# A planner for a hybrid encoder: TensorE's clock priced by activity, split copies and elementwise work free to change engine, leads for each layer and attention block

## The chip, the core and the metric

The kernel runs on one core of a Trainium2 chip. The metric is device time in microseconds (us) of one launch. The engines are TensorE (PE; PEld is its weight load), VectorE (DVE), ScalarE (ACT), GpSimd (POOL) and SyncE (SP, which here only issues transfers).

## What is computed

Two layers of an encoder over 512 tokens of width 1024, all in float32. Each layer has a mixer stage and a feed-forward stage:

```python
h = rms_norm(x, norm_mix[l]); proj = h @ w_in[l]          # 1024 x 3224
y_att = banded window attention(q, k, v)                  # 6 heads, 4 blocks of 128 queries
y_dn  = gated DeltaNet, one scan per direction            # 6 heads, 8 chunks of 64
y_rw  = RWKV-7, one scan per direction                    # 4 heads, 8 chunks of 64
x = x + concat(y_att, y_dn, y_rw) @ w_out[l]
h = rms_norm(x, norm_ffn[l])
x = x + (silu(gate) * val) @ w_down[l]                    # gate, val = conv3(h @ w_up[l])
```

Both recurrences are computed by chunks: inside each chunk a triangular matrix is inverted, and a scan of 8 dependent steps follows. A last RMSNorm closes the trunk.

## The kernel before, in words

Tiles hold channels on 128 partitions and the 512 tokens along the free axis. A large product is made in three float32r passes: each operand is split into a high part (a copy that rounds) and a low part (source minus high), and high x high, low x high and high x low are summed in PSUM. For weights, `weights` (its tiles: `wr` as loaded, `wh` high, `wl` low) loads four 128x128 blocks at a time, copies them on ACT and subtracts on POOL; each of the three tiles has three buffers. For activations, `split` writes `hh` and `hl`; in the feed-forward stage the gated result is split into two halves of a `p`, `cv` or `at` tile. A product of width 1024 is 24 matmuls of 128x512 (8 blocks, 3 passes), one of width 2816 is 66.

The mixer of a layer runs, in the order in which the program records it: 9 projections with `token_shift` (RWKV's inputs); `rwkv_prep` for two head pairs; `dn_gates`; `dn_proj` 0 to 2 (three projections each, with a conv of five taps on DVE); `invert`, the first inversion, 62 dependent instructions on DVE; `finish_inverse` 0, its PE part; `rwkv_scan`; `attn_proj` and `dn_prep` 0 to 2 beside it; `rwkv_out`; `invert_both`, the second inversion, 65 instructions on DVE; `finish_inverse` 1 and 2; `dn_scan`; `attn_head` 0 to 2 (four blocks each) and `gate_proj` 0 to 2 as filling; `dn_out`. After it come the output projection (`w_out`) and the feed-forward stage (up, down).

Nothing runs in the recorded order. Every call goes to a `Plan` (`add`), which notes its engine, its cost by a formula (`price`), its dependences and the tiles that it needs. `schedule` then places all 12326 calls: it takes the engine that is free first, and on it the ready call of the highest priority, where priority is the longest chain of costs behind the call plus a lead of its group, `LEAD`. A group is one call of a task such as `dn_prep`; before, both layers share a lead. `emit` writes the calls in the planned order, and the engines run their queues in that order, each queue strictly in sequence. So the plan decides what stands in front of what; how long it takes is decided on the chip. Every instruction shows line L516, the recorder's.

Three rules of the planner matter here. `other` names a second engine that may run a call; `schedule` offers the call to both and the one that is free first takes it. `admit` lets a tile be opened early if the memory allows. And the PE model in `schedule` doubles a matmul's cost after the PE has been idle.

Of the kernel before, what the change touches and what calls it, by code (L numbers as in the profile page):

```python
# [7 lines left out]
F32 = mybir.dt.float32  # L8
F32R = mybir.dt.float32r
# [89 lines left out]
def _param_array(inputs):  # L99
# [27 lines left out]
    "token_shift": 631900,  # L127
# [7 lines left out]
class Plan:  # L135
# [3 lines left out]
    def __init__(self, nc):  # L139
# [3 lines left out]
        self.flexible = True  # L143
        self.group, self.count, self.per_layer, self.lead = None, {}, {"proj": 9, "finish_inverse": 3, "rwkv_prep": 2, "dn_prep": 3, "dn_proj": 3, "attn_head": 3, "gate_proj": 3, "rwkv_out": 2, "dn_out": 3}, LEAD
# [8 lines left out]
    def task(self, f):  # L153


        def started(*a, **k):
            mine = self.group is None
            if mine:
                n = self.count[f.__name__] = self.count.get(f.__name__, -1) + 1
                name = f"{f.__name__}{n % self.per_layer[f.__name__]}" if f.__name__ in self.per_layer else f.__name__  # L160
            else:
                name = self.group
# [8 lines left out]
            def steps():  # L171
                while True:
                    old, self.group = self.group, name
# [94 lines left out]
    def other(self, o, name, reads, writes):  # L268

        if not self.flexible or not writes or len(reads) < 1 or "float32r" in str(writes[0].dtype) or reads[0].dtype != F32:  # L270
            return None
        dst, src = o.args[0], o.args[1]
        n = int(np.prod(dst.shape[1:]))
        psum = str(src.space).endswith("PSUM")
# [5 lines left out]
        if o.eng == "DVE" and name == "tensor_copy":  # L280
            return "ACT", self.nc.scalar.activation, (dst, src, AF.Copy), {}, 190 + 0.85 * n
# [1299 lines left out]
```

## Time and profile before

| what | value |
|---|---|
| median of 3 runs (lowest, highest) | 1678.78 us (1677.74, 1680.12) |
| profiled execution, its own time | 1681.65 us |
| span of the profile, first to last instruction | 1679.5 us |
| granted TensorE clock, mean | 0.946 |
| busy: PE, DVE, ACT, POOL | 91%, 64%, 44%, 38% |

The profiled execution is 2.9 us above the median, and 2.15 us of its time lie outside the span. A granted clock of 1.00 is 2.4 GHz, 0.50 is 1.2 GHz; a value between is a mean over both levels. Busy time of an engine counts its instructions; how near a stage is to its limit is seen when the busy time of an engine is set against the length of the same stretch.

### The profile page before, as it was taken

To read this page: it belongs to the slowest core of one execution; us is meant where nothing else is said; L and a number is where in the kernel's file an instruction comes from. 1 tells how busy PE (TensorE), PEld (TensorE's weight loads), DVE (VectorE), ACT (ScalarE), POOL (GpSimd) and SP (SyncE) were. 2 spreads that over 40 slices of the span, in tenths; PEclk is the share of its full clock that TensorE was granted. 3 is DMA by queue.
4 is the path that set the end of the run, shared out by engine and by line. 5 is a ranking of instruction groups with operands and counts; after the bars stand their busy time and mean duration, and the time that the engine had idled before them with its cause. 6 is when DMAs were issued, how large, how long until landed. Compare 5 with 4: busy or idle time off the path is not lost. (4 is left out here: it accounts for less than half of the span.)

```text
span 1679.5 us, 29012 instructions
## 1 busy us (share of the span) xinstructions
PE 1531.1 (91%) x11500; PEld 1192.8 (71%) x11500; DVE 1083.1 (64%) x1689; ACT 736.2 (44%) x1399; POOL 645.2 (38%) x510
## 2 busy tenths in 40 slices
PE   7999787589999999999999996966899999999996
PEld 5677665367777777788876775644677877777885
DVE  7799977967437666740058998789654566766101
ACT  5565345454543433332236544355544433334221
POOL 5422332010555554555552232410017454555553
PEclk9999889779999999999999997996799999999998
DMA  6312303010233333333342121120003333333332
GB/s 177 84 34 76 70 20 89 13 34 2 71 91 100 94 89 95 94 106 112 108 105 64 47 75 39 54 86 1 27 14 89 94 88 95 95 93 88 115 91 85
DMA packets 230536, 126.07 MB, mean 75 GB/s; under 512 B 23656, under 2 KB 221416, under 8 KB 230400
## 3 DMA queue, kind: packets, MB, share of 16 engines
q1 hardware_dynamic: 228624, 121.02, 25.8%
q10 hardware_dynamic: 1776, 3.20, 0.7%
q8 instruction: 90, 1.47, 0.3%
q14 instruction: 46, 0.38, 0.1%
HBM read 117.84 MB, written 6.34 MB: 74 GB/s over the span
## 5 line engine op out<-in xcount | busy, mean ns | idle before, releaser
L516 POOL TENSOR_TENSOR wl<-wr,wh 128x512 fp32r<-128x512 f32 (+1 forms) x408 | 558.1, 1379 | 830.1 <-ACT wh L516 667.9
L516 PE MATMUL ps<-hh,wh 128*128 128x512 f32 x1248 | 457.6, 399 | 6.9 <-ACT wh L516 6.9
L516 ACT ACTIVATE wh<-wr 128x512 fp32r<-128x512 f32 (+1 forms) x408 | 243.5, 616 | 495.9 <-PE ps L516 433.9
L516 PE MATMUL ps<-hh,wl 128*128 128x512 f32 x1248 | 452.9, 398 | 7.4 <-POOL wl L516 5.3
L516 PE MATMUL ps<-hl,wh 128*128 128x512 f32 x1248 | 451.6, 394 | 0.0
L516 PEld LDWEIGHTS ps<-hh,wl 128*128 128x128 f32 x1248 | 232.7, 187 | 84.2 <-POOL wl L516 30.3
L516 PEld LDWEIGHTS ps<-hh,wh 128*128 128x128 f32 x1248 | 233.6, 188 | 69.8 <-ACT wh L516 16.2
L516 PEld LDWEIGHTS ps<-hl,wh 128*128 128x128 f32 x1248 | 233.8, 188 | 51.7 <-issue 3.4
L516 DVE TENSOR_TENSOR p<-ps,p 128x512 f32<-128x512 f32 (+2 forms) x72 | 38.2, 551 | 197.4 <-PE ps L516 197.1
L516 PE MATMUL ps<-p,wh 128*128 128x512 f32 x512 | 158.2, 389 | 0.0
L516 DVE TENSOR_TENSOR td<-ps,rb 128x512 f32<-128x512 f32 (+1 forms) x64 | 43.7, 688 | 136.4 <-PE ps L516 136.3
L516 PEld LDWEIGHTS ps<-p,wh 128*128 128x128 f32 x512 | 96.1, 188 | 19.9
L516 DVE SCALAR_TENSOR_TENSOR tr<-td,fixed,tr 128x511 f32<-128x511 f32 x88 | 105.3, 1197 | 0.6 <-ACT tr L516 0.4
L516 PE MATMUL ps<-p,wl 128*128 128x512 f32 x256 | 99.8, 390 | 0.0
L516 ACT ACTIVATE p<-p 32x256 f32<-32x256 f32 (+3 forms) x112 | 66.0, 589 | 16.1 <-DVE p L516 11.2
L516 PE MATMUL ps<-fixed,cv 128*128 128x128 f32 x168 | 36.6, 338 | 38.8 <-ACT cv L516 35.7
L516 DVE SCALAR_TENSOR_TENSOR td<-tr,fixed,td 128x511 f32<-128x511 f32 x88 | 70.8, 805 | 0.3
L516 PE MATMUL ps<-p,p 32*32 32x32 f32 (+2 forms) x1232 | 56.1, 253 | 14.9 <-DVE p L516 11.3
L516 DVE TENSOR_TENSOR tr<-tr,td 128x512 f32<-128x512 f32 x44 | 67.3, 1529 | 1.6
L516 ACT ACTIVATE p<-ps 64x256 f32<-64x256 f32 (+4 forms) x113 | 44.9, 401 | 52.7 <-PE ps L516 33.3
L516 PEld LDWEIGHTS ps<-sm,p 64*64 64x64 f32 x1344 | 49.4, 145 | 24.6 <-DVE sm L516 12.9
L516 PEld LDWEIGHTS ps<-p,p 32*32 32x32 f32 (+1 forms) x1232 | 51.3, 143 | 21.5 <-DVE p L516 12.1
(170 smaller groups left out, 2089.5 us busy)
## 6 DMA issues: line engine op xcount, KB each, us to landing
wr<-ffn_w_up SPq DMA_DIRECT2D x176, 256.0 KB, 2.8
wr<-w_in SPq DMA_DIRECT2D x88, 256.0 KB, 2.8
wr<-ffn_w_down SPq DMA_DIRECT2D x80, 256.0 KB, 2.9
p<-scr ACTq DMA_DIRECT2D x12, 256.0 KB, 5.1
wr<-w_in SPq DMA_DIRECT2D x24, 128.0 KB, 2.6
wr<-w_out SPq DMA_DIRECT2D x32, 96.0 KB, 2.6
wr<-w_out SPq DMA_DIRECT2D x16, 192.0 KB, 2.6
p<-xt SPq DMA_DIRECT2D x8, 256.0 KB, 4.5
```

The source lines that it names most:

```text
L516: tc.keep_in_program_order(call(*args, **kw))
```

## The change

It changes only the planner, its table of leads and one argument.

1. **The clock in the plan.** The rule "idle for over 5 us, then slow until enough full-width work is done" goes. Instead the plan books PE time by beats of fixed length, each matmul weighted by its kind, and doubles costs in a beat that follows one with too little. This changes the plan only; nothing on the chip is set.
2. **Who may change engine** (`other`). Before, a call that writes float32r could not. Now the high copies of weights and activations may go from ACT to DVE, and a `tensor_tensor` in SBUF with two dimensions and at least 128 elements in a row may go from DVE to POOL or back. The low part of the weights has three dimensions and stays on POOL.
3. **Leads** for each layer (`a`, `b`), and for each block of an attention head; `token_shift` 0 to 7 get their own.
4. `wake` puts a call that is still blocked back on the waiting list. `admit` tests the name instead of the size of a room; the rooms below 4 are the same three, so nothing changes by it. `bufs=2` to `bufs=1` in `split` has no effect: `Plan.tile` uses `bufs` only for tags in its `room`, and `hh` and `hl` are not among them.

```diff
 LEAD = {
-    "attn_head0": -17500, "attn_head1": 13500, "attn_head2": 4300, "attn_proj": 281000, "dn_gates": 100400, "dn_out0": 5100,
...
+    "attn_head0a.0": 28600, "attn_head0a.1": -100, "attn_head0a.2": -158900, "attn_head0a.3": 800, "attn_head0a.4": 1500, "attn_head0b.0": 50500,
...
@@ other
-        if not self.flexible or not writes or len(reads) < 1 or "float32r" in str(writes[0].dtype) or reads[0].dtype != F32:
+        if not writes or not reads:
             return None
...
-        if o.eng == "DVE" and name == "tensor_copy":
+        if o.eng == "DVE" and name == "tensor_copy" and src.dtype == F32:
...
+        if name == "tensor_tensor" and not psum and n >= 128 and len(dst.shape) == 2 and o.eng in ("DVE", "POOL"):
+            e, f, cost = ("POOL", self.nc.gpsimd, 180 + 2.3 * n) if o.eng == "DVE" else ("DVE", self.nc.vector, 165 + 1.04 * n)
+            return e, f.tensor_tensor, o.args, o.kw, cost
@@ schedule
-                if t - free[e] > self.COLD:
-                    cold, heat = True, 0.0
-                if cold:
+                while t >= edge:
+                    slow = here < (self.UP if slow else self.DOWN) * self.BEAT
+                    here, then, edge = then, 0.0, edge + self.BEAT
+                if slow:
                     cost *= 2
...
-            elif o.contend and e == "DVE" and free["POOL"] > t:
+            elif e == "DVE" and (o.contend or o.eng == "POOL") and free["POOL"] > t:
                 cost += min(cost, free["POOL"] - t)
```

The set of calls is the same in both kernels; 470 of ACT's calls now run on DVE (176 before), 60 of DVE's on POOL and 15 of POOL's on DVE. Three places show the new order.

**First, DVE in layer 0, between the RWKV scan and the second inversion.** `p_105` is RWKV's result (task `rwkv_out`), `p_538` to `p_541` belong to `dn_prep` 2. Before:

```order
L516 TENSOR_TENSOR p_538<-p_538,fixed 128x1024 x2
L516 TENSOR_TENSOR p_105<-p_105,tr_558 128x512
L516 TENSOR_SCALAR p_105<-p_105,fixed 128x512
L516 TENSOR_TENSOR p_105<-p_105,tr_553 128x512
L516 TENSOR_TENSOR p_105<-p_105,tr_554 128x512
L516 TENSOR_TENSOR cv_398<-cv_398,td_532 128x512
L516 SCALAR_TENSOR_TENSOR cv_408<-cv_408,td_533 128x512
```

DVE in the changed kernel:

```order
L544 TENSOR_TENSOR p_538<-p_538,fixed 128x1024 x2
L544 SCALAR_TENSOR_TENSOR cv_408<-cv_408,td_533 128x512
L544 COPY p_529<-ps_531 64x4x64 x3
L544 TENSOR_TENSOR p_540<-ps_542,p_538 128x512
L544 TENSOR_SCALAR p_105<-p_105,fixed 128x512
L544 TENSOR_TENSOR p_541<-ps_542,p_538 128x512
```

The three products and sums on `p_105` and that on `cv_398` have left DVE; they stand on POOL now.

**Second, DVE in the up projection of layer 0.** `td` and `tr` are the two halves of a step (multiply by the norm, three taps), `p_1020` the split result, `wh` the high weights of the next blocks. Before, one step:

```order
L516 TENSOR_TENSOR td_1028<-ps_1021,rb_848 128x512
L516 TENSOR_TENSOR tr_1018<-ps_1011,rb_848 128x512
L516 TENSOR_SCALAR td_1019<-tr_1018,fixed 128x512
L516 SCALAR_TENSOR_TENSOR tr_1029<-td_1028,fixed,tr_1029 128x511
L516 SCALAR_TENSOR_TENSOR td_1019<-tr_1018,fixed,td_1019 128x511
L516 SCALAR_TENSOR_TENSOR tr_1029<-td_1028,fixed,tr_1029 128x511
L516 SCALAR_TENSOR_TENSOR td_1019<-tr_1018,fixed,td_1019 128x511
L516 TENSOR_TENSOR tr_1010<-tr_1010,td_1019 128x512
L516 TENSOR_TENSOR p_1020<-tr_1010,p_1020 128x512
```

In the changed kernel:

```order
L544 CAST wh_1035<-wr_1034 128x512
L544 CAST wh_1042<-wr_1041 128x512
L544 TENSOR_TENSOR td_1028<-ps_1021,rb_848 128x512
L544 TENSOR_SCALAR tr_1029<-td_1028,fixed 128x512
L544 SCALAR_TENSOR_TENSOR tr_1029<-td_1028,fixed,tr_1029 128x511 x2
L544 CAST wh_1051<-wr_1050 128x512
L544 TENSOR_TENSOR tr_1018<-ps_1011,rb_848 128x512
L544 TENSOR_SCALAR td_1019<-tr_1018,fixed 128x512
L544 SCALAR_TENSOR_TENSOR td_1019<-tr_1018,fixed,td_1019 128x511 x2
L544 TENSOR_TENSOR tr_1010<-tr_1010,td_1019 128x512
L544 CAST p_1020<-tr_1010 128x512
L544 TENSOR_TENSOR p_1020<-tr_1010,p_1020 128x512
```

Copies (CAST) of weights and of the result have joined the queue; over the whole up projection 44 of the 88 weight copies and 20 of the 22 result copies are on DVE.

**Third, PE in layer 0, the last gate projection** (`ps_687`, `gate_proj` 2). Before, it stands among the last `dn_prep` transposes and the first attention scores, at the start of the second inversion:

```order
L516 MATMUL ps_687<-hh_88,wl_690 128x512
L516 MATMUL ps_545<-fixed,cv_398 128x128 x3
L516 MATMUL ps_669<-at_436,at_490 128x384
L516 MATMUL ps_687<-hh_92,wh_692 128x512
L516 MATMUL ps_687<-hl_93,wh_692 128x512
L516 MATMUL ps_670<-at_436,at_490 128x384
```

In the changed kernel it stands in the DeltaNet scan (`ps_708`, `ps_710`, both tiles of the scan), behind the second of its steps:

```order
L544 MATMUL ps_710<-p_541,sm_683 64x64 x2
L544 MATMUL ps_687<-hh_77,wh_689 128x512
L544 MATMUL ps_708<-sm_686,cv_253 64x64 x4
L544 MATMUL ps_708<-sm_686,cv_331 64x64 x4
L544 MATMUL ps_708<-sm_686,cv_398 64x64 x4
L544 MATMUL ps_687<-hl_78,wh_689 128x512
L544 MATMUL ps_687<-hh_77,wl_690 128x512
```

From the last two rows on, 23 matmuls of the projection follow one another, then 20 of attention, and only then the scan goes on. The second inversion has lost a projection that ran beside it, and the scan has gained one.

## Rows read from the trace of the kernel before

**Rows 1.** The page: busy time and share of each engine, and PE's granted clock by 40 slices.

```profile
PE 1531.1 (91%) x11500; PEld 1192.8 (71%) x11500; DVE 1083.1 (64%) x1689; ACT 736.2 (44%) x1399; POOL 645.2 (38%) x510
...
PEclk9999889779999999999999997996799999999998
```

**Rows 2.** Windows, layer 0: stretch, length, busy (instructions) by engine, PEclk, DMA share, GB/s.

```profile
13.00:84.00 71.00, 68.51 (x278) 49.03 (x279) 56.08 (x67) 38.68 (x69) 33.87 (x24) 1.00 0.41 107
84.00:145.00 61.00, 56.83 (x765) 45.94 (x765) 56.28 (x81) 39.30 (x80) 11.54 (x7) 1.00 0.20 54
145.00:198.00 53.00, 46.00 (x307) 37.15 (x303) 50.91 (x81) 17.95 (x34) 21.61 (x17) 0.94 0.32 75
198.00:211.00 13.00, 7.43 (x188) 6.38 (x183) 10.74 (x19) 9.55 (x23) 0.63 (x1) 0.50 0.09 23
211.00:271.00 60.00, 52.63 (x732) 38.95 (x732) 40.77 (x79) 21.20 (x38) 21.29 (x29) 0.93 0.21 47
271.00:297.00 26.00, 18.89 (x175) 13.32 (x176) 24.55 (x41) 18.93 (x39) 1.28 (x1) 0.87 0.23 67
297.00:351.00 54.00, 35.12 (x278) 22.21 (x276) 50.87 (x108) 25.87 (x70) 4.12 (x4) 0.75 0.04 11
351.00:362.00 11.00, 8.29 (x265) 7.83 (x266) 7.68 (x21) 7.30 (x18) 1.27 (x1) 0.56 0.25 62
362.00:424.00 62.00, 57.67 (x1017) 44.97 (x1014) 38.49 (x118) 26.59 (x79) 5.04 (x6) 0.91 0.04 13
424.00:434.00 10.00, 9.91 (x39) 6.86 (x38) 6.76 (x11) 7.78 (x14) 2.96 (x2) 1.00 0.19 52
...
478.00:724.00 246.00, 243.44 (x1045) 194.10 (x1044) 164.50 (x189) 96.26 (x153) 124.06 (x87) 1.00 0.32 92
```

**Rows 3.** Windows, layer 1: first inversion, `dn_prep`, second inversion; columns as in Rows 2.

```profile
973.00:1025.00 52.00, 45.10 (x317) 35.93 (x313) 50.02 (x78) 17.10 (x32) 21.53 (x17) 0.96 0.33 77
...
1095.00:1123.00 28.00, 19.54 (x179) 14.04 (x180) 24.70 (x40) 19.70 (x39) 1.46 (x1) 0.88 0.34 99
1123.00:1177.00 54.00, 35.18 (x278) 22.22 (x276) 50.72 (x108) 25.85 (x70) 4.07 (x4) 0.75 0.04 11
```

**Rows 4.** Chain that ended last, its longest piece: start us, us, what.

```profile
1537.46 126.82 PE ps L516 x558
```

**Rows 5.** Timeline of DVE, 276 to 292 us: RWKV's result (`p<-p,tr`, `p<-p,fixed` 128x512).

```profile
278.34 1.63 DVE L516 TENSOR_TENSOR p<-p,tr 128x512 f32<-128x512 f32 x1 [0.72 <-ACT tr L516]
280.01 0.55 DVE L516 TENSOR_SCALAR p<-p,fixed 128x512 f32<-128x512 f32 x1
280.59 1.42 DVE L516 TENSOR_TENSOR p<-p,tr 128x512 f32<-128x512 f32 x2
```

**Rows 6.** Groups of DVE, second inversion of layer 0: count, busy us, mean ns.

```profile
L516 DVE CUSTOM_DVE_ANT_0 cv<-ps,fixed 128x384 f32<-128x384 f32 x5 | 3.0, 609 | 0.0
```

**Rows 7.** Groups of DVE, POOL and ACT, up projection of layer 0 (478 to 724 us).

```profile
L516 DVE TENSOR_SCALAR td<-tr,fixed 128x512 f32<-128x512 f32 x19 | 9.7, 513 | 0.7
...
L516 POOL TENSOR_TENSOR wl<-wr,wh 128x512 fp32r<-128x512 f32 x87 | 124.9, 1446 | 124.2 <-ACT wh L516 110.8 <-PE ps L516 12.8 <-issue 0.6
...
L516 ACT ACTIVATE wh<-wr 128x512 fp32r<-128x512 f32 x87 | 52.8, 629 | 109.6 <-PE ps L516 109.3
```

**Rows 8.** Timeline, up projection: the same operation beside POOL and without it.

```profile
606.82 1.78 DVE L516 SCALAR_TENSOR_TENSOR tr<-td,fixed,tr 128x511 f32<-128x511 f32 x1
...
609.18 0.74 DVE L516 SCALAR_TENSOR_TENSOR tr<-td,fixed,tr 128x511 f32<-128x511 f32 x1
...
603.55 1.29 POOL L516 TENSOR_TENSOR wl<-wr,wh 128x512 fp32r<-128x512 f32 x1 [3.17 <-ACT wh L516]
605.32 2.73 POOL L516 TENSOR_TENSOR wl<-wr,wh 128x512 fp32r<-128x512 f32 x2 [0.47 <-PE ps L516]
```

**Rows 9.** Timeline, start: the transfer of the positions and its conversion on DVE.

```profile
9.89 0.42 SPq L516 DMA_DIRECT2D td<-positions  x1
...
21.70 1.52 DVE L516 CAST td<-td 128x512 f32<-128x512 int32 x1
```

More of the change, by code (lines that the diff above doesn't have):

```diff
@@ L142, in __init__ @@
         self.room = {"ps": 8, "sb": 148000, "wr": 3, "wh": 3, "wl": 3}
-        self.flexible = True
-        self.group, self.count, self.per_layer, self.lead = None, {}, {"proj": 9, "finish_inverse": 3, "rwkv_prep": 2, "dn_prep": 3, "dn_proj": 3, "attn_head": 3, "gate_proj": 3, "rwkv_out": 2, "dn_out": 3}, LEAD
+        self.group, self.count, self.per_layer, self.lead = None, {}, {"proj": 9, "finish_inverse": 3, "token_shift": 8, "rwkv_prep": 2, "dn_prep": 3, "dn_proj": 3, "attn_head": 3, "gate_proj": 3, "rwkv_out": 2, "dn_out": 3}, LEAD
     def tile(self, pool, shape, dtype, tag, bufs, name):
@@ L158, in started @@
             if mine:
-                n = self.count[f.__name__] = self.count.get(f.__name__, -1) + 1
-                name = f"{f.__name__}{n % self.per_layer[f.__name__]}" if f.__name__ in self.per_layer else f.__name__
+                n, m = self.count.get(f.__name__, -1) + 1, self.per_layer.get(f.__name__, 1)
+                self.count[f.__name__] = n
+                name = f"{f.__name__}{n % m}" + "ab"[n // m]
             else:
@@ L171, in steps @@
             def steps():
+                i = 0
                 while True:
-                    old, self.group = self.group, name
+                    old, self.group = self.group, f"{name}.{i}" if mine and f.__name__ == "attn_head" else name
+                    i += 1
                     try:
@@ L273, in other @@
         n = int(np.prod(dst.shape[1:]))
-        psum = str(src.space).endswith("PSUM")
+        psum = any(str(x.space).endswith("PSUM") for x in reads + writes)
         if o.eng == "ACT" and name == "activation" and o.args[2] == AF.Copy and set(o.kw) <= {"scale"}:
@@ L329, in price @@
         return n
-    SWITCH, STAY, COLD, WARM = 150, 300, 5000, 4000
+    SWITCH, STAY = 150, 300
+    BEAT, DOWN, UP = 3413.0, 0.44, 0.8
+    WEIGHT = {"full": 1.0, "half": 0.8, "q64": 0.9, "q32": 0.2}
     def admit(self, t):
@@ L338, in admit @@
         turn, line = self.turn[r], self.line[r]
-        if line[turn] == t or self.room[r] < 4:
+        if line[turn] == t or r[0] == "w":
             return line[turn] == t
@@ L385, in schedule @@
         avail = {e: [] for e in engines}
-        last, cold, heat, dma_free, releases = None, False, 0.0, 0.0, []
+        last, slow, here, then, edge, lit, dma_free, releases = None, False, 0.0, 0.0, self.BEAT, 0.0, 0.0, []
         push, pop = heapq.heappush, heapq.heappop
@@ L405, in wake @@
         def wake(r, t):
-            for h, e in held[r]:
-                push(heaps[e], (max(t, h.ready), h.n))
-            held[r] = []
+            was, held[r] = held[r], []
+            for h, e in was:
+                if h.done:
+                    continue
+                still = blocked(h)
+                if still is None:
+                    push(heaps[e], (max(t, h.ready), h.n))
+                else:
+                    held[still].append((h, e))
         order = []
@@ L483, in schedule @@
                 last = o.mode
-                if t - free[e] > self.COLD:
-                    cold, heat = True, 0.0
-                if cold:
+                while t >= edge:
+                    slow = here < (self.UP if slow else self.DOWN) * self.BEAT
+                    here, then, edge = then, 0.0, edge + self.BEAT
+                if slow:
                     cost *= 2
-                    heat += cost if o.mode == "full" else 0
-                    cold = heat < self.WARM
-            elif o.contend and e == "DVE" and free["POOL"] > t:
+                w, a, b = self.WEIGHT[o.mode], max(t, lit), t + cost + 150
+                if b > a:
+                    here += w * max(0.0, min(b, edge) - a)
+                    then += w * max(0.0, b - max(a, edge))
+                    lit = b
+            elif e == "DVE" and (o.contend or o.eng == "POOL") and free["POOL"] > t:
                 cost += min(cost, free["POOL"] - t)
@@ L676, in split @@
     def split(src, gcol, tag, k):
[L677 to L678 removed]
+        hi = plan.tile(bp, [P, T], F32R, tag=f"hh{k}", bufs=1, name=nm("hh"))
+        lo = plan.tile(bp, [P, T], F32R, tag=f"hl{k}", bufs=1, name=nm("hl"))
         if gcol is None:
```

3 lines of the change are left out of this document (removed), and 21 rows, old and new, of the table LEAD.

## Prediction

> **What bounds the kernel now.** I read the page's busy times first: PE is busy for 91% of the span, at a granted clock that falls at two places, once in each layer's mixer [rows 1]. The chain that ended last says which engine holds the end: one unbroken piece of 126.8 us of PE [rows 4]. Then I cut layer 0 into stages with windows, because a mean over 1680 us says nothing about a stage [rows 2]. There are three kinds.
>
> In the feed-forward stage PE is the limit: 1045 matmuls in 246 us, busy for 243.4 of them, 0.235 us for each [rows 2]. Nothing that relieves another engine can save more than the 2.6 us that are idle there.
>
> In four mixer stretches DVE is the limit: 84 to 145 us (56.3 of 61 us busy), the first inversion (50.9 of 53), `dn_prep` between RWKV's scan and the second inversion (24.6 of 26) and the second inversion (50.9 of 54) [rows 2]. Layer 1 shows the same for the last three: 50.0 of 52, 24.7 of 28, 50.7 of 54 [rows 3]. An instruction that leaves DVE here shortens the stretch by its whole time, one that comes in lengthens it.
>
> The rest are chains: the two scans (40.8 of 60 and 38.5 of 62 us of DVE) and `finish_inverse` (198 to 211 and 351 to 362 us), where PE runs at a granted clock of 0.50 and 0.56, the 1.2 GHz level for most of it, after inversions that left it short of work [rows 2]. Here order matters more than load.
>
> **The change part by part.** I counted the instructions of both orders stage by stage and priced them from rows; the sum is made against the profiled execution's 1681.65 us and then carried to the median, which lies 2.9 us lower.
>
> *Start.* The positions are now loaded first. Their issue costs SP 0.42 us ahead of the input, and DVE's first instruction is their conversion, 1.52 us [rows 9]. In return the rotary tables leave a stretch in which PE is busy for 68.5 of 71 us [rows 2], so they free little. Between +1.5 and -1: I take **+0.5 us**.
>
> *Before the first inversion.* In layer 0, 12 matmuls of `dn_proj` 1 move behind its first instruction (12 x 0.235 = 2.8 us of PE) and 13 small ones come forward. PE (56.8 of 61) and DVE are both near their limit there [rows 2], so I take half, -1.4. Layer 1 moves 2 such matmuls back and 15 small ones forward: +0.5. Its 13 weight copies on DVE fall early, where DVE is busy for 56 of 71 us in layer 0 [rows 2]; they cost nothing unless that gap is gone, and then 13 x 0.51 = 6.7 us [rows 7]. Together **-0.9 us**, from -3 to +7.
>
> *First inversion.* In layer 0 DVE gets 6 instructions more (83 for 77), of `dn_proj` 2, about 4.8 us; 5 of `dn_proj` 1 no longer stand behind the inversion, but that stretch waits for the slow PE, and I count 2.3 of them. Layer 1 keeps its 76. **+2.5 us**, from -1 to +4.8.
>
> *Between RWKV's scan and the second inversion.* In layer 0 DVE's count falls from 39 to 32. RWKV's six products and sums go to POOL; three of them held DVE for 1.63 + 1.42 us [rows 5], so six for about 5 to 6, and one `dn_prep` product of 0.7 goes too; some of `dn_prep` 1 moves into the scan. The sum is 8.4 us, and as parts of it only move to the scan I take -5.5 (from -8.4 to -2). POOL needs 1.3 to 1.4 us for each [rows 8], but is busy for 1.3 of 26 us there [rows 2], and only the output projection waits for them. In layer 1, five go and as many attention instructions come in: -1 (from -2.5 to +2). **-6.5 us.**
>
> *Second inversion.* Layer 0 gets 4 instructions more on DVE (100 for 96), +1.3; layer 1 has 12 fewer (84 for 96), most of an attention block whose scores cost 0.61 us each [rows 6] beside small ones, -4.3. **-3 us**, from -5.5 to +1.
>
> *DeltaNet's scan.* DVE's instructions fall from 106 to 95 and 97, by about 6 us in each layer, but DVE is busy for only 38.5 of 62 us [rows 2], so I credit half, -3. Against that stands the last gate projection: 23 matmuls in one run are 5.4 us of PE, in front of the scan's next matmuls. A step waits for PE, then DVE, then PE, so part of the run falls in a gap that the scan has anyway; I take +1.5. That is -1.5 in each layer, **-3 us**, from -13 to +11 for both.
>
> *After the scan.* Before it ends, layer 0 has done 4 of the output projection's matmuls where there were 18, so 14 x 0.235 = 3.3 us more PE work is left. But `dn_out` is a chain with gaps: its 10 us hold 25 such matmuls, 5.9 us [rows 2]. I take **+1 us**, from -2 to +3.3.
>
> *Feed-forward stage.* ACT loses 44 of 88 weight copies and 20 result copies in each up projection, at 0.63 us each [rows 7]; ACT was busy for 96 of 246 us [rows 2], so nothing is gained. DVE gets 64 copies, 2.9 for each of 22 steps. Their cover is DVE's room: it is busy for 164.5 of 246 us, so of a step of 11.2 us some 3.7 us are free [rows 2]. The nearest row is DVE's scaling of the same size, 0.513 us [rows 7], so 2.9 copies need 1.5 us and stay hidden: **0 us**. At the other end a copy could wait for one whole subtraction of POOL, 1.29 us [rows 8]: 2.9 x 1.8 = 5.2 us, 1.5 more than there is, 66 us over 44 steps. I take the near end, since the row holds 19 such instructions of this very stage.
>
> That last point is where a page speaks against the change. The trace: the same DVE instruction takes 1.78 us when POOL works at its start and 0.74 us when it does not [rows 8]. The Trainium skill ("SBUF — State Buffer", section "SBUF: two separate sides") says that VectorE, in a two-port mode or with two SBUF inputs, and GpSimd take one pair of ports as an exclusive lock, the second to come waiting for the whole instruction of the first. By that rule each new copy either waits for a subtraction or holds one up, and the end of 5.2 us would be the common case; the 0.513 us of the scalings say that the instruction rarely comes second.
>
> The terms: 0.5 - 0.9 + 2.5 - 6.5 - 3 - 3 + 1 + 0 = **-9.4 us**, 0.6%. From 1678.78 that gives **1669 us**.
>
> **The rivals.**
>
> *The clock is won too* (faster). If the new order keeps PE at the 2.4 GHz level where it was slow, PE's part of those stretches shrinks: 7.4 x 0.50 = 3.7 us in the first `finish_inverse`, 8.3 x 0.44 = 3.6 in the second, 57.7 x 0.09 = 5.2 in the scan [rows 2], 12.5 us in each layer. For it speaks that the first inversion has 187 large matmuls beside it where it had 170; against it that the second loses 16 of 40. Three quarters of it on top of my sum: 1650 us.
>
> *Nothing moves* (the same). The stretches turn out to be set by dependences, DVE's gaps only grow: 1679 us. For it speaks that each stretch keeps its long tasks in the same sequence; against it that DVE was busy for 94 to 96% of three of them [rows 2].
>
> *The copies fill DVE in the feed-forward stage* (slower). They go behind multiplications that wait for PSUM, and beside POOL. Below 3.7 / 2.9 = 1.28 us for a copy nothing is seen; every 0.1 us above costs 0.29 x 44 = 13 us. At 1.45 us it is +22, with my sum 1691 us.
>
> *The scan pays for the projection* (slower). If both runs stand wholly in the chain, that is 10.8 instead of 3 us, and DVE's 6 us of credit fall away too; with 3 us more after the scan, 1686 us.
>
> **How the numbers follow.** A measurement of this kernel can tell about 0.2% from no change, 3.4 us. My forecast gets 0.40, with a range of its own from 1661 to 1675; the clock 0.22; nothing 0.16; the copies 0.13; the scan 0.09. That is 0.62 faster, 0.16 the same, 0.22 slower. The range runs from 1645, most of the clock's gain, to 1691, the first slower rival at its price; it leaves out the best of the first and the worst of the third case, some 2 in 10.
>
> **What would show it.** Right: 271 to 297 us of layer 0 is 5 us shorter, the second inversion of layer 1 4 us shorter, the up projection still 246 us with DVE busy for some 197, its copies at 0.5 to 0.8 us. Wrong: copies above 1.28 us and PE idle behind `wh`; a scan of more than 64 us; granted clocks near 1.00 in the two `finish_inverse` stretches, which would make me too cautious.

## The result and the profile after

| | before | after |
|---|---|---|
| median of 4 runs (lowest, highest) | 1678.66 us (1677.74, 1680.12) | 1752.32 us (1750.51, 1755.31) |
| span of the profile | 1679.5 us | 1748.7 us |
| granted TensorE clock, mean | 0.946 | 0.942 |

The changed kernel takes 1.044 times the time of before (95% interval 1.0422 to 1.0458): 73.7 us slower, where 9 us faster was forecast, and 61 us above the upper end of the range. 69.2 us of it lie in the span.

The page of the changed kernel: busy times, granted clock, and the groups around the weight copies (`wh` the high part, `wl` the low part; the last column is the engine's idle time just before them and what ended it).

```profile
PE 1541.1 (88%) x11500; PEld 1186.9 (68%) x11500; DVE 1267.3 (72%) x1938; ACT 565.9 (32%) x1105; POOL 701.9 (40%) x555
...
PEclk9999989579999999999999997986899999999999
...
L544 PE MATMUL ps<-hh,wh 128*128 128x512 f32 x1248 | 475.4, 399 | 36.2 <-ACT wh L544 17.9
...
L544 DVE CAST wh<-wr 128x512 fp32r<-128x512 f32 (+1 forms) x215 | 136.2, 637 | 230.5 <-PE ps L544 197.9
...
L544 ACT ACTIVATE wh<-wr 128x512 fp32r<-128x512 f32 x193 | 120.1, 628 | 490.6 <-PE ps L544 452.7
```

The same groups before, when ACT made all 408 copies:

```profile
L516 PE MATMUL ps<-hh,wh 128*128 128x512 f32 x1248 | 457.6, 399 | 6.9 <-ACT wh L516 6.9
...
L516 ACT ACTIVATE wh<-wr 128x512 fp32r<-128x512 f32 (+1 forms) x408 | 243.5, 616 | 495.9 <-PE ps L516 433.9
```

Against [rows 1], DVE has 184 us more work and PE is busy for 88 instead of 91%. The copies on DVE take 0.64 us each, as hoped. The column behind is the news: DVE stands idle for 230.5 us right in front of them, 197.9 of that until a matmul ends. A copy needs a free `wh` buffer, and while it waits at the head of the queue, everything behind it on DVE waits too. ACT waited in the same way before, but ACT is the less loaded of the two (736 us of work, DVE 1083 [rows 1]).

Windows of the changed kernel, cut at its own stage starts, layer 0 and then layer 1 (columns as in [rows 2]).

```profile
0.00:160.00 160.00, 132.65 (x1008) 98.92 (x1008) 123.67 (x161) 85.75 (x162) 61.31 (x47) 0.96 0.32 88
160.00:217.00 57.00, 47.70 (x306) 38.57 (x307) 53.41 (x85) 15.73 (x26) 25.60 (x20) 0.95 0.30 70
217.00:227.00 10.00, 7.50 (x222) 6.78 (x216) 5.96 (x16) 7.45 (x16) 0.00 (x0) 0.50 0.01 3
227.00:290.00 63.00, 57.47 (x788) 41.80 (x787) 44.73 (x82) 20.91 (x45) 31.13 (x34) 0.94 0.20 54
290.00:310.00 20.00, 13.06 (x117) 8.15 (x118) 18.59 (x31) 14.55 (x31) 7.93 (x5) 1.00 0.33 100
310.00:367.00 57.00, 34.59 (x238) 20.48 (x239) 53.21 (x113) 23.65 (x63) 6.57 (x6) 0.64 0.02 5
367.00:380.00 13.00, 9.04 (x310) 8.47 (x306) 8.81 (x20) 8.63 (x18) 2.54 (x2) 0.54 0.22 64
380.00:441.00 61.00, 54.16 (x987) 43.06 (x983) 35.46 (x107) 25.19 (x71) 12.62 (x12) 0.96 0.04 11
...
503.00:755.00 252.00, 239.19 (x1025) 188.33 (x1024) 203.92 (x245) 56.16 (x88) 117.38 (x87) 1.00 0.31 89
```

```profile
1088.00:1151.00 63.00, 56.09 (x743) 41.08 (x743) 46.06 (x87) 22.15 (x46) 23.27 (x29) 0.92 0.16 45
1151.00:1180.00 29.00, 16.99 (x169) 9.41 (x167) 26.00 (x46) 22.67 (x50) 9.51 (x7) 0.83 0.14 35
1180.00:1230.00 50.00, 31.18 (x282) 19.82 (x283) 45.52 (x91) 17.63 (x48) 2.76 (x3) 0.65 0.07 20
...
1244.00:1303.00 59.00, 54.70 (x988) 43.21 (x990) 37.64 (x110) 25.55 (x72) 12.61 (x12) 0.96 0.08 24
```

The up projection is 252 us for 246, with PE idle for 12.8 us where it was 2.6, and it does 1025 matmuls in that time for 1045 [rows 2]. By stage, from the first and last DVE instruction of each task in both traces (layer 1 counted from its first matmul):

| stage | layer 0, us | layer 1, us | together | forecast |
|---|---|---|---|---|
| begin to first inversion | 145.5 to 159.6 | 132.5 to 144.2 | +25.8 | -0.4 |
| first inversion with its PE part | 67.1 to 67.7 | 66.5 to 68.4 | +2.5 | +2.5 |
| RWKV's scan | 58.9 to 62.7 | 56.2 to 63.4 | +11.0 | no term |
| scan to second inversion | 26.0 to 20.1 | 27.9 to 28.5 | -5.3 | -6.5 |
| second inversion with its PE part | 64.9 to 70.2 | 65.2 to 63.7 | +3.8 | -3 |
| DeltaNet's scan | 62.1 to 61.1 | 62.5 to 59.6 | -3.9 | -3 |
| scan's end to the next layer or the end | 415.7 to 434.1 | 425.0 to 441.9 | +35.3 | +1 |

Sum: +69.2. These lengths come from one profiled execution of each kernel. Three kernels with one order (before, slots_before, slots_six_before) differ by up to 2 us in a mixer and 3 us in a single stage of it, so smaller differences say little. Below, "mixer" is all up to the end of DeltaNet's scan (+16.9 us in each layer) and "feed-forward" the last line (+18.4 and +16.9).

Two places show how it happens. Timeline of the changed kernel, start: DVE, and PE's wait.

```profile
9.09 3.09 DVE L544 SCALAR_TENSOR_TENSOR hl<-p,fixed,hh 128x512 fp32r<-128x512 f32 x2
12.10 2.66 DVE L544 TENSOR_SCALAR td<-td 128x512 f32<-128x512 f32 x2
14.80 5.03 DVE L544 SCALAR_TENSOR_TENSOR td<-td,td 128x512 f32<-128x512 f32 x3
19.86 1.37 DVE L544 TENSOR_SCALAR td<-td 128x512 f32<-128x512 f32 x1
21.27 0.69 DVE L544 SCALAR_TENSOR_TENSOR td<-td 128x512 f32<-128x512 f32 x1
21.88 3.40 DVE L544 SCALAR_TENSOR_TENSOR hl<-p,fixed,hh 128x512 fp32r<-128x512 f32 x5
...
22.68 0.50 PE L544 MATMUL ps<-hl,wh 128*128 128x512 f32 x1 [3.53 <-DVE hl L544]
```

Seven instructions of the rotary tables (`td`), and not one, stand ahead of the splits (`hl`) for which PE waits, from 12.1 to 22.0 us.

Timeline of the changed kernel, up projection of layer 0: ACT, and PE's wait.

```profile
601.52 0.74 DVE L544 SCALAR_TENSOR_TENSOR tr<-td,fixed,tr 128x511 f32<-128x511 f32 x1
...
602.29 0.63 ACT L544 ACTIVATE tr<-tr 128x512 f32<-128x512 f32 x1
...
602.83 0.61 ACT L544 ACTIVATE wh<-wr 128x512 fp32r<-128x512 f32 x1
...
603.50 0.50 PE L544 MATMUL ps<-hh,wh 128*128 128x512 f32 x1 [1.43 <-ACT wh L544]
```

DVE's instruction ends at 602.26, ACT's `tr<-tr` starts at 602.29, the weight copy behind it at 602.83, and PE has run dry. The pattern comes back every 36 us, about three steps.

### The profile page after: what moved, and what is told of

It is laid out like the page before. It is cut to its first block, busy times and chain, and to the rows that moved or that the text cites. A ratio compares the mean times of both kernels' runs of the same rounds, so it can differ in the third digit from the quotient of the medians.

```text
span 1748.7 us, 28992 instructions
## 1 busy us (share of the span) xinstructions
PE 1541.1 (88%) x11500; PEld 1186.9 (68%) x11500; DVE 1267.3 (72%) x1938; ACT 565.9 (32%) x1105; POOL 701.9 (40%) x555
## 3 DMA queue, kind: packets, MB, share of 16 engines
q10 hardware_dynamic: 1776, 3.20, 0.7%
## 5 line engine op out<-in xcount | busy, mean ns | idle before, releaser
L544 POOL TENSOR_TENSOR wl<-wr,wh 128x512 fp32r<-128x512 f32 (+1 forms) x408 | 544.7, 1343 | 708.9 <-ACT wh L544 247.8
L544 PE MATMUL ps<-hh,wh 128*128 128x512 f32 x1248 | 475.4, 399 | 36.2 <-ACT wh L544 17.9
L544 PE MATMUL ps<-hh,wl 128*128 128x512 f32 x1248 | 465.3, 399 | 4.7 <-POOL wl L544 4.2
L544 PE MATMUL ps<-hl,wh 128*128 128x512 f32 x1248 | 465.9, 394 | 3.5 <-DVE hl L544 3.5
L544 DVE CAST wh<-wr 128x512 fp32r<-128x512 f32 (+1 forms) x215 | 136.2, 637 | 230.5 <-PE ps L544 197.9
L544 ACT ACTIVATE wh<-wr 128x512 fp32r<-128x512 f32 x193 | 120.1, 628 | 490.6 <-PE ps L544 452.7
L544 DVE SCALAR_TENSOR_TENSOR tr<-td,fixed,tr 128x511 f32<-128x511 f32 x88 | 82.4, 938 | 1.9 <-ACT tr L544 0.4
L544 ACT ACTIVATE p<-p 32x256 f32<-32x256 f32 (+3 forms) x104 | 62.5, 602 | 36.8 <-DVE p L544 34.0
L544 ACT ACTIVATE tr<-p 128x512 f32<-128x512 f32 x46 | 28.7, 628 | 126.5 <-DVE p L544 115.9
L544 PE MATMUL ps<-sm,p 64*64 64x64 f32 x1344 | 61.7, 234 | 6.7 <-DVE sm L544 6.1
```

Of the source, the lines that this page charges most:

```text
L544: tc.keep_in_program_order(call(*args, **kw))
```

## The experiments

Each ratio is to the kernel before, run on the same chip; its median there lies between 1678.7 and 1682.5 us, so small differences between rows are better read from the ratios. clock_only, leads_only, engines_only and old_leads were timed twice, the others four times. "Mixer" and "feed-forward" are the stages of layer 0 and layer 1 in the profile, as defined above.

| run | us | ratio (interval) | mixer, us | feed-forward, us |
|---|---|---|---|---|
| before | 1678.66 | 1 | 424.5, 410.8 | 415.7, 425.0 |
| after | 1752.32 | 1.0440 (1.0422 to 1.0458) | 441.4, 427.7 | 434.1, 441.9 |
| copies_back | 1745.97 | 1.0373 (1.0332 to 1.0413) | 443.0, 428.0 | 432.5, 437.3 |
| products_back | 1758.91 | 1.0451 (1.0416 to 1.0485) | 443.5, 428.9 | 434.8, 445.2 |
| old_engines | 1760.40 | 1.0452 (1.0417 to 1.0488) | 458.3, 428.3 | 432.3, 436.4 |
| old_order_new_engines | 1730.77 | 1.0281 (1.0247 to 1.0315) | 446.3, 430.7 | 420.1, 429.6 |
| clock_only | 1717.31 | 1.0224 (1.0194 to 1.0254) | 441.3, 428.5 | 414.7, 426.6 |
| leads_only | 1738.90 | 1.0353 (1.0311 to 1.0394) | 445.2, 431.8 | 421.9, 432.6 |
| engines_only | 1762.28 | 1.0492 (1.0461 to 1.0522) | 453.1, 440.7 | 426.1, 437.6 |
| old_leads | 1758.74 | 1.0471 (1.0440 to 1.0501) | 447.7, 441.6 | 425.6, 439.2 |
| copies_early | 1752.13 | 1.0425 (1.0404 to 1.0447) | 442.8, 425.8 | 433.8, 440.0 |
| tables_late | 1759.81 | 1.0474 (1.0451 to 1.0498) | 445.5, 428.8 | 435.7, 443.8 |
| no_copy_rule | 1738.04 | 1.0347 (1.0327 to 1.0367) | 439.7, 441.1 | 421.6, 430.0 |
| no_product_rule | 1739.05 | 1.0352 (1.0333 to 1.0370) | 447.4, 427.9 | 424.7, 434.4 |
| slots_after | 1715.16 | 1.0194 (1.0179 to 1.0209) | 443.0, 428.3 | 413.4, 423.9 |
| slots_early | 1709.41 | 1.0159 (1.0143 to 1.0174) | 445.2, 425.7 | 410.5, 419.9 |
| begin_leads | 1765.91 | 1.0499 (1.0482 to 1.0517) | 440.2, 438.1 | 434.3, 445.5 |
| slots_before | 1657.33 | 0.9851 (0.9836 to 0.9866) | 424.6, 408.8 | 403.4, 415.7 |
| nudged_price | 1696.35 | 1.0093 (1.0074 to 1.0112) | 430.3, 417.2 | 415.2, 425.8 |
| slots_six_before | 1657.20 | 0.9854 (0.9832 to 0.9876) | 425.1, 410.8 | 402.9, 414.8 |

**Engines or order?** Theory Q: the new engines carry the loss. Theory L: the new order does. The order stays as it is and only the engine of a call is put back, in `emit`:

```diff
+            if o.eng == "ACT" and o.run == "DVE" and "wh" in o.args[0].tensor.name:
+                o.run = o.eng
             call, args, kw = (o.call, o.args, o.kw) if o.run == o.eng else o.alt[1:4]
```

> The changed kernel with its order kept; only the weight copies (wr to wh) that its planner gave to DVE run on ACT again, each at its place in the order. Theory Q (engines): a copy waits for its turn in DVE's queue, behind elementwise instructions that wait for PE, and POOL and PE wait for the copy; PE's idle time behind wh falls from 36 to under 10 us, the up projections go back from 252 to 246 us each, and the mixers gain as well: 1700 to 1720 us. Theory L (order): most of the loss is in the mixers and comes from the new order; only the feed-forward stages come back, 15 to 25 us: 1727 to 1737 us. Theory S (shared port): the copies also slow POOL's subtraction and the other way round; then POOL's mean for wl falls by 0.1 us or more. In the trace POOL's mean is already lower than before the change (1.34 for 1.45 us), so I expect no gain from it.

> The changed kernel with its order kept; only the two-operand elementwise instructions that changed between DVE and POOL run on their old engine, each at its place. Theory Q: the products on POOL make DVE's products beside them longer (p<-tr,p takes 1.47 us in layer 0 before the first inversion, 0.67 in the kernel before), so the time falls, by 10 to 20 us: 1732 to 1742 us, most of it between 89 and 159 us and in its twin of layer 1. Theory L: POOL's products relieved DVE and the order was laid out for that; on DVE again they lengthen the stretches that DVE bounds, and the time rises by 5 to 15 us: 1757 to 1767 us.

Here the condition is `{o.eng, o.run} == {"DVE", "POOL"}`. In the next two, `moved` lists the calls that the other kernel runs on their second engine:

```diff
+            o.run = o.alt[0] if o.n in moved else o.eng
```

> The changed kernel's order with each instruction on the engine that it had before the change. It shows what the new order alone does. Theory Q: nearly all of the 73 us goes: 1680 to 1700 us. Theory L: the order holds most of it: 1715 to 1740 us. An order that was laid out for other engines can cost of itself, 10 us or so, which this run cannot tell from a bad order.

> The order of the kernel before, with each instruction on the engine that the change gave it. It shows what the engines alone do. Theory Q: most of the 73 us: 1725 to 1750 us, with PE idle behind wh for some 30 us. Theory L: only the feed-forward part, 15 to 30 us: 1695 to 1710 us.

On the new order the engines matter little: 6 us back with the copies (11 by the ratios), nothing that can be told apart with the products, nothing with all engines as before. POOL's mean for `wl` is 1.355 us with the copies back and 1.343 without, so theory S adds nothing. On this order, then, the loss stays whichever engines are used, and it is larger than theory L gave. But the new engines on the old order cost 48 us too (1730.77 against 1682.5 on that chip). The two do not add up: the order alone costs 78 us, the engines alone 48, both together 74. How much of the first two is a misfit, an order and a set of engines that were not laid out for each other, these runs cannot tell. Theory Q falls as an explanation of the whole.

**Which part of the planner?** The change has three: price of the clock (P), table of leads (T), rules for engines. Each was tried alone, and two of them without the leads. Each edit is one hunk of the change (its first line stands for it), made or taken back. The fourth part, `wake`, stays in all four; planned with `wake` alone, the old planner gives the old list, call for call, so it is no cause there.

```diff
 clock_only: before with
-                if t - free[e] > self.COLD:
+                while t >= edge:
 leads_only: before with
-    "attn_head0": -17500, "attn_head1": 13500, ...
+    "attn_head0a.0": 28600, "attn_head0a.1": -100, ...
 engines_only: before with
-        if not self.flexible or not writes or len(reads) < 1 or "float32r" in str(writes[0].dtype) or reads[0].dtype != F32:
+        if not writes or not reads:
 old_leads: after with
-    "attn_head0a.0": 28600, "attn_head0a.1": -100, ...
+    "attn_head0": -17500, "attn_head1": 13500, ...
```

> The planner with its old leads and its old rules for other engines; only the rule by which it prices TensorE's clock is the new one. Theory P (the price of the clock): the new price alone makes it lay the mixers out differently, and that holds a good part of the loss that the swaps of engines in place did not show: 1700 to 1725 us. Theory T (the table of leads): without the new leads the price does little: 1675 to 1690 us.

> The planner with its old price of the clock and its old rules for other engines; only the table of leads is the new one (a lead for each layer and each block). Theory T: the new leads hold most of the loss: 1725 to 1760 us, with the stretch up to the first inversion 5 us longer in layer 0 and 10 in layer 1, as in the changed kernel. Theory P: 1675 to 1700 us. The leads were written for the other two rules, so a part of what this run loses may be a misfit and not the leads' own.

> The planner with its old leads and its old price of the clock; only the rules for other engines are the new ones, so that it lays the order out itself for copies on DVE and products on POOL. In the order of before, with these engines put in place, it was 1731 us. Theory Q (engines): DVE's and POOL's queues carry the loss in any order: 1720 to 1740 us. Theories P and T: an order laid out for them takes most of it away: 1680 to 1700 us.

> The changed kernel with the old leads: the new price of the clock and the new rules for other engines stay. Theory T: most of the 73 us goes: 1685 to 1705 us. Theories P and Q: little goes: 1730 to 1755 us.

Each part alone loses: 2.2, 3.5 and 4.9%. P and T each forecast the run of their own part rightly, Q set its part too low; as every part loses alone, no single one of them is the cause. The rules for engines cost most, and they do it in the mixers (+28.6 and +29.9 us) as well as in the feed-forward stages (+10.4 and +12.6). With both new rules, the new leads gain some 6 us (`old_leads` against after, with intervals that overlap). The parts lose in different places: layer 1's stretch up to the first inversion is 132.5 us before and 132.7 in clock_only, but 139.9 in leads_only and 144.2 in old_order_new_engines, as in the changed kernel; clock_only loses 14.6 us in the two second inversions.

**The feed-forward stages.** Theory W: copies wait for their turn in the queue. Theory Q': an order laid out for two copying engines is the cost, in place or not.

```diff
 copies_early:
+    for each wh copy on ACT or DVE: pass up to 2 earlier calls of its engine,
+    but no call that it depends on, no other wh copy, and no call that frees its buffer
 no_copy_rule, in other:
+        if o.eng == "ACT" and "float32r" in str(writes[0].dtype): return None
 no_product_rule, in other:
-        if name == "tensor_tensor" and not psum and ...
```

> The changed kernel on the same engines; only 57 of its 408 weight copies (43 on ACT, 14 on DVE) stand one or two instructions earlier in their engine's queue, ahead of elementwise instructions that wait for another engine, as far as a slot for the copy is free there. Theory W (the turn in the queue): in the up projections ACT's copy stands behind tr<-tr, which waits for DVE, and PE waits 1.4 us for the copy every four steps; those gaps go: PE's idle time behind wh falls from 36 to 20 us or less, each up projection is 4 to 8 us shorter, the whole 1735 to 1745 us. Theory D (the copies take DVE's time, or the ports): nothing changes, 1750 to 1755 us.

> The changed kernel, planned again without the rule that lets copies of ACT go to DVE when they write float32r (the weight copies among them); the leads, the price of the clock and the products between DVE and POOL stay. Theory Q' (an order laid out for two copying engines is the cost in the feed-forward stages, in place or not): these go back to some 417 us from the end of DeltaNet's scan to the next layer's first projection, from 434, in both layers, and the whole takes 1715 to 1725 us. If the products between DVE and POOL are the cost: 1745 to 1755 us.

> The changed kernel, planned again without the rule that lets two-operand instructions change between DVE and POOL; the leads, the price of the clock and the copies on DVE stay. Theory Q': the feed-forward stages stay at 430 us and more, the mixers change by less than 10 us each: 1740 to 1765 us. If the products are the cost: 1710 to 1725 us.

The group of matmuls behind a new `wh`, first in copies_early, then in no_copy_rule:

```profile
L574 PE MATMUL ps<-hh,wh 128*128 128x512 f32 x1248 | 475.9, 400 | 27.7 <-DVE wh L574 13.8
```

```profile
L544 PE MATMUL ps<-hh,wh 128*128 128x512 f32 x1248 | 461.3, 400 | 12.8 <-ACT wh L544 6.7
```

Theory W fails alone: 8.5 us less idle time behind `wh`, no time gained. Q' holds in part for the copies: planned without them, the feed-forward stages lose 12.5 and 11.9 us of their excess (less than forecast), but layer 1's mixer is 13.4 us longer, and the whole misses both forecasts. That the products would do nothing there is wrong; without their rule 9.4 and 7.5 us come back. As either rule taken away also draws the list anew, what each rule costs of itself is not shown. In layer 0's mixer the products do what the forecast said: without them the stretch to the second inversion is 24.8 instead of 20.1 us, with them put back in place (products_back) 22.7. In layer 1 they do not: it is 17.3 us without their rule and 28.5 with it.

What can the order have that survives when the copies go back to ACT? Theory H: it keeps weight buffers occupied. There are three each; in the changed kernel the longest `wl` is held for 22 us.

```diff
-            hi = plan.tile(bp, [P, WK, m], F32R, tag="wh", bufs=3, name=nm("wh"))
-            lo = plan.tile(bp, [P, WK, m], F32R, tag="wl", bufs=3, name=nm("wl"))
+            hi = plan.tile(bp, [P, WK, m], F32R, tag="wh", bufs=4, name=nm("wh"))
+            lo = plan.tile(bp, [P, WK, m], F32R, tag="wl", bufs=4, name=nm("wl"))
```

The planner still books three, so the order is the same.

> The changed kernel with the same order and engines; only the split weights (wh and wl) have four buffers each instead of three. Theory H (the order of the matmuls holds buffers): in the up projection of layer 0, 19 of 78 wl tiles are held for over 14 us, the longest for 22 us (before the change 1 of 76, the longest for 14.6), so a copy gets its buffer late and PE waits for it; with a fourth buffer that wait goes: from the end of DeltaNet's scan to the next layer 422 to 428 us for 434, in both layers, and 1735 to 1742 us in all. If the copies are late for their place in the queue, or the buffers only move the wait to the queue: 1747 to 1754 us.

> As the run before, with four buffers for wh and wl, and the copies one or two instructions earlier in their queues as far as these four buffers allow. Theory H: the two waits stood behind each other (earlier places alone gave nothing); together they give 420 to 426 us from the end of DeltaNet's scan to the next layer and 1725 to 1737 us in all. If neither buffer nor queue is the cause: 1747 to 1755 us.

> The kernel before the change with four buffers for wh and wl instead of three, the order kept. Theory H says that its order holds buffers short (8.3 us on average, 13.3 at most for wh), so little waits there: PE is idle behind wh for 6.9 us in all. 1672 to 1679 us; a gain of 3 us or more would show that buffers bound it too.

Groups of slots_after, then of slots_before:

```profile
L544 PE MATMUL ps<-hh,wh 128*128 128x512 f32 x1248 | 473.4, 398 | 12.2 <-DVE wh L544 4.4
...
L544 ACT ACTIVATE wh<-wr 128x512 fp32r<-128x512 f32 x193 | 118.6, 625 | 318.8 <-PE ps L544 137.7
L544 DVE CAST wh<-wr 128x512 fp32r<-128x512 f32 (+1 forms) x215 | 129.5, 618 | 118.8 <-PE ps L544 66.0
```

```profile
L516 ACT ACTIVATE wh<-wr 128x512 fp32r<-128x512 f32 (+1 forms) x408 | 235.6, 609 | 180.9 <-PE ps L516 85.9
```

Theory H holds, and more strongly than expected: the changed kernel is 37 us faster, 20.7 and 18.0 of it in its feed-forward stages, and DVE's idle time in front of the copies falls from 230.5 to 118.8 us. Now the earlier places help as well, by 6 us. The kernel before gains too, 1.5%, although its PE was idle behind `wh` for only 6.9 us: with four buffers its feed-forward stages are 12.3 and 9.3 us shorter. In layer 0's stage, 58 of its 1776 large matmuls had started 0.3 to 0.6 us after the one ahead, where 0.227 is usual; that is 11 us more than usual, and it does not show as idle; with four buffers it is 11 of them. Compared at four buffers, the feed-forward stages of the two kernels differ by 10.0 and 8.2 us instead of 18.4 and 16.9: 17 of the 35 us are waits for buffers that the new order adds.

**The beginnings.** Theory B takes the tables for the wait at the start, theory T the leads of layer 1's first projections.

```diff
 tables_late, in emit:
+        late = [o for o in order if o.group == "rotary_tables0a" and o.start < 30000]
+        (placed behind the last call that writes hl35)
 begin_leads:
-    "proj2b": -353000, "proj3b": 81700, ... "token_shift1b": -1075800, ...
+    "proj3b": -46800, ... "token_shift0b" to "token_shift7b": 631900
```

> The changed kernel with the rotary tables of its start (the load of the positions and the 11 instructions on DVE and ACT that follow from it) behind hl35, the last split of the input, instead of ahead of it. Theory B (begin): the input lands later behind the positions, and PE waits at 19 to 23 us for hl18, which stands behind these instructions on DVE; the first inversion starts 5 to 8 us earlier and the whole takes 1744 to 1748 us. If the tables only fill DVE's gaps, the same instructions are in the way elsewhere: 1750 to 1755 us.

> The changed kernel with the old leads for the projections (proj1 to proj8) and the token shifts of layer 1 alone; up to 875 us its order is the same. Theory T: the new leads put proj2 and its token shift last (it ends 60 us into the layer, 18 in the kernel before), RWKV's preparation begins 14 us later and PE waits 6 us in one piece; with the old leads layer 1's first inversion starts 133 to 137 us after the layer's begin instead of 144, and the whole takes 1741 to 1746 us. If other leads or the engines hold that stretch: 142 us or more, 1750 us or more.

Both fail. Timeline of tables_late, PE and ACT:

```profile
30.32 0.79 PE L550 MATMUL ps<-hh,wh 128*128 128x512 f32 x1 [7.36 <-ACT wh L550]
```

```profile
26.80 0.63 ACT L550 ACTIVATE fixed<-td 128x512 f32<-128x512 f32 x1 [2.29 <-DVE td L550]
27.52 0.72 ACT L550 ACTIVATE fixed<-td,fixed 128x512 f32<-128x512 f32 x1
28.25 1.28 ACT L550 ACT_TABLE_LOAD   x1
29.54 0.20 ACT L550 ACTIVATE fixed<-fixed 128x2 f32<-128x2 f32 x1
29.65 0.61 ACT L550 ACTIVATE wh<-wr 128x512 fp32r<-128x512 f32 x1
```

The wait for `hl18` is gone, and a longer one has taken its place: ACT's part of the tables now waits for DVE, with a weight copy behind it. In begin_leads RWKV's preparation of the first head pair begins 22 us into layer 1 instead of 38, that of the second pair 47 instead of 28: the two have changed places, and the first inversion still starts at 144 us.

What becomes of a wait that is taken away is seen in DVE's waits of layer 1 up to the first inversion, changed kernel (875 to 1020 us), then slots_after (856 to 999 us): waited for, us in total, times, longest.

```profile
DVE wh L544 <- PE ps L544: 13.6, 9, 3.3
DVE p L544 <- ACT p L544: 9.3, 7, 3.0
```

```profile
DVE tr L544 <- PE ps L544: 10.0, 5, 3.2
DVE p L544 <- ACT p L544: 9.5, 8, 3.0
...
DVE wh L544 <- issue: 1.0, 1, 1.0
```

A fourth buffer takes 12.6 us of waits away from DVE there, and the stretch is 1.5 us shorter: another wait, of 10.0 us, has come in. The mixers' loss is not the buffers': they take 443.0 and 428.3 us with four, 441.4 and 427.7 with three.

**Any new order?** Theory F: the old leads were fitted to one order, and any other order loses. One constant of the old planner is nudged:

```diff
-            o.cost = 190 + 0.85 * n + (60 if o.kw.get("accum_out") is not None else 0)
+            o.cost = 190 + 0.86 * n + (60 if o.kw.get("accum_out") is not None else 0)
```

> The kernel before the change with one constant of its planner nudged: ACT's price per element 0.86 instead of 0.85, some 5 ns of 600 for a whole tile. No rule, lead or engine choice of the change is in it, but the list is drawn anew from it and the order parts from the old one early. Theory F (the old leads were fitted to one order, and any other loses): 10 us or more in each mixer, 1695 to 1725 us. If the content of the change costs the mixers their time: within 6 us of the kernel before, 1673 to 1686 us.

> The kernel before the change, its order kept, with six buffers each for wh and wl and four for the loaded weights instead of three. With four for wh and wl it was 1657 us, and the feed-forward stages were then within 7 us of matmuls back to back. Theory H: little is left there, 1650 to 1657 us. If the loads can now run ahead through the mixers as well, up to 10 us more: 1645 us.

The nudge, with nothing of the change in it, costs 0.93% (0.74 to 1.12). 5.8 and 6.4 us are in the mixers, less than expected; the feed-forward stages hold. So theory F is right for about a third of the mixers' 16.9 us. The other 10 to 11 us in each came with every part of the change that was tried, and on old engines as well; which positions they hang on stays open. One nudge is one draw, too; another may lose more or less, and it did not change the order alone: the planner also chose other engines for some calls (DVE has 1663 instructions, ACT 1425, for 1689 and 1399 [rows 1]). Six buffers give no more than four.

## Why the prediction was wrong

Three of its terms for counted moves came out near their size in sum: first inversion +2.5 (measured +2.5), scan to second inversion -6.5 (-5.3), DeltaNet's scan -3 (-3.9). The first of them is luck: it was forecast for layer 0, and came as 0.6 us there and 1.9 in layer 1, where nothing was expected. In the second, layer 0's -5.9 was forecast as -5.5, but the products on POOL account for 2.6 of it (products_back), and layer 1 became 0.6 us longer where -1 was forecast.

Of the signs it named, three came: 271 to 297 us became 5.9 us shorter, layer 1's second inversion 3.7 us, the copies in the up projection stayed far below 1.28 us. The fourth did not: the up projection takes 252 us instead of 246, with DVE busy for 203.9 and not some 197. One sign that it had set against itself came too: PE is idle behind `wh` for 36.2 us, 6.9 before.

The sum was 78.6 us too low: 34.3 in the feed-forward stages, 26.2 before the first inversions, 11.0 in RWKV's scan, 6.8 in the second inversions, the rest within 1.2 us a stage. The failing steps are these.

1. **"Feed-forward stage: 0 us" and "after the scan: +1".** Measured +35.3. The cover was worked out as DVE's free time, 3.7 us of a step, against 2.9 copies of 0.5 to 1.8 us; the copies took 0.74 us (row below) and would have fitted. What was left out is where a copy stands: behind elementwise work that waits for another engine, and in front of other work while it waits for one of three buffers. The runs give 17 us to buffers (slots_after against slots_before) and 7 to places in the queue (slots_early; with three buffers the earlier places gave nothing). 32 matmuls more were left after the scans, 14 and 18, at 0.227 us apiece 7.3 us; the forecast had named that for layer 0 as up to 3.3 us. Some 4 us stay without a name.

2. **"Start: +0.5".** It priced the conversion and one DMA issue. PE's first matmul starts 1.0 us later, PE then waits 3.53 us in one piece for a split behind seven table instructions, and `proj` 8 starts 8.1 us later. That the tables cost those 8.1 us is not shown: with them behind the splits (tables_late) PE waits 7.36 us for a weight copy, and the first inversion starts 3.7 us later still.

3. **"Before the first inversion: -0.9", "13 weight copies cost nothing".** Layer 1's stretch is 11.7 us longer, layer 0's some 6 beyond the start. In layer 1 the 13 copies take 7.3 us on DVE, about the 6.7 that were set as the bad end, and the 13.6 us for which DVE stands in front of them were in no term. But on this order neither is what holds the stretch: it takes 144.2 us, 142.6 with the copies back on ACT (copies_back) and 142.7 with a fourth buffer (slots_after). New leads alone and new engines alone each lengthen it (139.9 and 144.2 us, above); by what wait stays open.

4. **No term for RWKV's scan.** Parts of attention, `dn_prep` 1 and the gate projections were moved into it, 12 instructions on DVE in each layer where there was 1; others left it (DVE has 80 in all for 81 in layer 0, 86 for 78 in layer 1). PE is busy for 57.5 instead of 52.6 us in layer 0 [rows 2], and it is 3.8 us longer; layer 1 has 7.2. Filling that was moved into a chain was priced for DeltaNet's scan and not here; no run takes it out again, so that it is the cause is argued.

5. **"Second inversion: -3".** Measured +3.8. DVE's instructions were priced, +1.3 and -4.3 for the two layers; the inversions alone changed by +2.9 and -3.7. PE's part behind them had no term, and it is 2.5 and 2.2 us longer, at about the granted clock of before (0.54 and 0.56, for 0.56 in both). Why stays open.

6. **The premise below them all**, said only in the rival "nothing moves": that a stretch keeps its tasks in a sequence that is as good as the old one, so that counts of moved instructions price it. nudged_price shows how little slack this order has: one price changed by 1% costs 15 us.

Of the rivals, "the copies fill DVE" had the place and the sign, but its mechanism and so its threshold were wrong: PE waited with copies of 0.74 us. The clock was not won: the finishing stretches still run at 0.50 and 0.54, the second inversions fell from 0.75 to 0.64 and 0.65, with 35 and 31 us of PE work in them.

Groups of DVE in the changed kernel's up projection (503 to 755 us), against [rows 7], and two copies 0.6 us apart (DVE, then POOL beside them):

```profile
L544 DVE CAST wh<-wr 128x512 fp32r<-128x512 f32 x42 | 31.2, 744 | 37.6 <-PE ps L544 37.6
...
L544 DVE TENSOR_SCALAR td<-tr,fixed 128x512 f32<-128x512 f32 x7 | 10.8, 1546 | 0.2
```

```profile
607.56 0.43 DVE L544 CAST wh<-wr 128x512 fp32r<-128x512 f32 x1 [0.75 <-PE ps L544]
608.19 1.50 DVE L544 CAST wh<-wr 128x512 fp32r<-128x512 f32 x1 [0.20 <-PE ps L544]
...
608.12 1.28 POOL L544 TENSOR_TENSOR wl<-wr,wh 128x512 fp32r<-128x512 f32 x1 [3.04 <-DVE wh L544]
```

The rule that was weighed in the prediction (the Trainium skill, "SBUF — State Buffer", section "SBUF: two separate sides") agrees with this: 0.43 us alone, 1.50 us when POOL began 0.07 us earlier. Of DVE's 243 copies of 128x512 from float32 to float32r in the changed kernel, the 159 that began while POOL ran no product took at most 0.43 us; the 84 that began beside one took 0.42 to 1.55, half of them over 1.2. So a single copy can pay for POOL, and the scaling's 0.513 us [rows 7] was luck of that order: it is 1.55 us now. But that price was not what cost the time, since the copies back on ACT give only 6 us (11 by the ratios).

## What to carry to other kernels

Where engines run their queues in sequence, an instruction that is moved can cost more than its duration: while it waits at the head of its queue, all that stands behind it waits too. Read the idle time in front of its group, and not its mean alone. Before such a kernel's order is tuned, look for what makes it sensitive; here a fourth buffer for two tiles gave 1.5% on the old order and 37 us, half of the loss, on the new one, more than any change of leads that was tried. And an order that was fitted to one planner can be lost when a rule of the planner changes: measure the change against a nudge that means nothing.

The best version is the kernel before with four buffers for `wh` and `wl`: 1657.33 us, 0.9851 (0.9836 to 0.9866) of before.

## What was not expected of the hardware

- Short waits between matmuls do not show as idle time. The kernel before has PE busy for 243.4 of 246 us in its up projection [rows 2], and the feed-forward stage around it still became 12.3 us shorter with a fourth buffer. The count of matmuls in a stretch tells it where the busy share does not.
- The same copy on DVE takes 0.43 us when POOL runs no product at its start, and up to 1.55 us when it does; seven scalings of the up projection take 1.546 us, where 19 of them took 0.513 [rows 7], with no change of their own.
